# Matmul operand tiles moved to another address modulo 512 bytes by padding two small tiles

## The chip, the cores and the metric

One core of one Trainium2 chip runs the whole program. The metric is the device time of one execution in microseconds (us), as the median of several runs. The profile comes from one further execution with the hardware profiler on.

## What is computed

Two layers of a decoder trunk on 512 tokens with 1024 channels, all in float32. Cut to what matters here:

```python
# layer 0: a state-space head group (A) and a windowed attention head group (B)
hn   = rms_norm(h, mix_norm_w[0]);  proj = hn @ hyb_w_in[0]
y_a  = ssd_mixer(proj[..., :IN_A], ...)              # 1024 wide, gated and normalised
y_b  = swa_sink_attention(proj[..., IN_A:], ...)     # 16 heads of 64
h    = h + concatenate([y_a, y_b]) @ hyb_w_out[0]
# layer 1: a convolution module
h    = h + conformer_conv_module(rms_norm(h, mix_norm_w[1]), ...)
# after each layer, a gated MLP with a causal convolution of width 3
u    = causal_depthwise_conv(rms_norm(h, ffn_norm_w[i]) @ w_up, conv_w, conv_b)   # 1024 -> 5632
h    = h + (silu(u[..., :2816]) * u[..., 2816:]) @ w_down                         # 2816 -> 1024
```

## The kernel before, in words

**Tiling.** Activations lie with channels on the 128 partitions and the 512 tokens along the free axis, so a tile of 128 channels is 128 x 512 floats, 2048 bytes in each partition. A matrix product (`gemm`, L130 to L138) takes one output tile of 128 channels. Each operand is split into a high and a low part of the type fp32r, and a product of two operands is three matmuls of 512 columns that add into one PSUM bank: weights high by activations high (L135), weights high by activations low (L136), weights low by activations high (L137). The weights are the stationary operand, which a LDWEIGHTS brings into the array; the activations are the moving one, which streams past it.

**Weights.** `wload` (L123) fetches 128 x 1024 floats by DMA into `wr`, ScalarE makes the high part `wh` (L119) and VectorE the low part `wl` (L120). There are three buffers of each.

**Phases.** `mix` (layer 0's mixer), `ffn0`, `conf` (the convolution module) and `ffn1` follow each other. Tiles that all phases use (`wr`, `wh`, `wl`, `xr` and some more, L76) live in a pool that stays; each phase opens a pool of its own (L1094 to L1096) on top of it, and gives it back at its end. Inside a pool, tiles lie one after another in the order in which their names first appear, each beginning at a multiple of 32 bytes.

**The moving operands that matter here.** Three names hold them:

- `xr`, 16 tiles in the lasting pool: the normalised activations that enter all up-projections and input projections, and, in the second half of the output projection of `mix`, the operands of head group A (`ya`, L746 to L750).
- `att`, 16 tiles in the pool of `mix`: the split attention output `yb` (L698 to L702), the operands of the first half of that output projection. `out_half` (L754) multiplies one half for one of 8 output tiles: 8 operands x 3 matmuls = 24 matmuls. The first halves of tiles 0 to 4 are done first, in the banks `mm`, `mm`, `mm`, `pa`, `pa`; then the second halves of these, and then for tiles 5 to 7 a first and a second half each.
- `g`, 44 tiles in the pool of an `ffn` phase: the split gated activations (L796 to L799), the operands of the down-projection (L802 to L805). A down-projection has 8 output tiles x 22 operands x 3 = 528 matmuls, and there are two of them. In the phase `conf` the names `g`, `dg` and `u4` hold split operands of the last product (`u4` appears as `u` in the profile).

**Where these tiles lie.** The built program gives every tile a start address in the partition. Taken modulo 512 bytes:

```
tile                          before   with the change
wh, wl (stationary)               32          32
xr                                32          32
att (phase mix)                   64          32
g (phases ffn0 and ffn1)         224          32
g, dg, u4 (phase conf)            32          32
```

A `gemm` takes slices of 128 floats = 512 bytes of `wh` and `wl`, so every stationary slice has the same address modulo 512 as its tile. The pool of a phase begins at 123424 bytes, which is 32 modulo 512. In `ffn0` and `ffn1` its first tile is the table of convolution parameters, 176 floats = 704 bytes, and `g` follows. In `mix` it begins with `rows_t` (2048 bytes), two tiles `sel` (512 bytes each) and `warm` (one float, which takes 32 bytes), and `att` follows; after `att` come the other tiles of the phase (`par_mix`, `pairs`, `halves`, `bc`, `kv`, `xs`, `c`, `a` or `lt`, `b`, `d`, `bt` and small ones).

Of the kernel before, what the change touches and what calls it, by code (L numbers as in the profile page):

```python
# [10 lines left out]
AF = mybir.ActivationFunctionType  # L11
# [3 lines left out]
P = 128  # L15
# [43 lines left out]
def kernel(ctx: ExitStack, tc: tile.TileContext, x, w_in, w_dt, w_out,  # L59
                             pw1, pw2, w_up0, w_up1, w_dn0, w_dn1, par, cst, btab, out):  # L60
    nc = tc.nc
    V, S, G, TE = nc.vector, nc.scalar, nc.gpsimd, nc.tensor
# [16 lines left out]
    def sbt(tag, bufs, n=T, dt=F32, shape=None):  # L79
        pool = sb if tag in base else phase[0]  # L80
        return pool.tile(shape or [P, n], dt, name=nm(tag), tag=tag, bufs=bufs)
# [3 lines left out]
    def bank_of(tag):  # L85
        return ps.tile([P, T], F32, name=nm(tag), tag=tag, bufs=BANKS[tag])
# [5 lines left out]

    def pload(group, pool, queue=nc.scalar):
        a, b = PGROUP[group]
        room = 640 if group == "conf" else b - a
        ptiles[group] = pool.tile([P, room], F32, name=f"par_{group}")[:, : b - a]
        queue.dma_start(ptiles[group], par[:, a:b])

    pload("norm", one)

    def con(name):
# [10 lines left out]
    ones = one.tile([P, P], F32, name="ones")  # L112
# [17 lines left out]
    def gemm(bank, w, ops, first, last):  # L130
        wh, wl = w
        n = len(ops)
        for i, (xh, xl) in enumerate(ops):
            c = slice(i * P, (i + 1) * P)
            TE.matmul(bank, wh[:, c], xh, start=first and i == 0, stop=False)  # L135
            TE.matmul(bank, wh[:, c], xl, start=False, stop=False)  # L136
            end = TE.matmul(bank, wl[:, c], xh, start=False, stop=last and i == n - 1)  # L137
        return end  # L138
# [85 lines left out]
    def mixer(norm, nxt):  # L224
        mk = lambda shape, name, dt=F32: phase[0].tile(shape, dt, name=name)
# [94 lines left out]

        first, ws, banks = [], [], {}
        with tc.manual_schedule():
            warm = mk([P, 1], "warm")
            S.activation(warm, ones[:, 0:1], AF.Exp)
            idle = bank_of("pc")
            for _ in range(9):
                TE.matmul(idle[:, :P], ones, ones, start=True, stop=True)
            wd = sbt("att", 16)[:, : KD * 16].rearrange("p (k m) -> p k m", k=KD)
            S.dma_start(wd, w_dt)
            raws = [sbt("wr", 3, RING) for _ in range(3)]  # L330

            def wpart(i, p):
                if i == len(raws):
                    raws.append(sbt("wr", 3, RING))
                nc.sync.dma_start(raws[i][:, p], w_in[i][:, p])

            lower, upper, whole = slice(0, RING // 2), slice(RING // 2, RING), slice(0, RING)
            xload = lambda k: nc.sync.dma_start(h[k], x[:, k, :])
            xload(0)
            wpart(0, lower)  # L340
            xload(1)
            wpart(0, upper)
            xload(2)
            wpart(1, whole)
            for k in (3, 4, 5):
                xload(k)
            wpart(2, whole)
            for k in (6, 7):
                xload(k)
            wd2 = sbt("att", 16, T, F32R).rearrange("p (k m) -> p k m", k=KD)  # L350
            V.memset(f32(wd2), 0.0)
            V.tensor_copy(wd2, f32(wd2))
            V.tensor_copy(wd2[:, :, 0:16], wd)
            V.tensor_tensor(wd2[:, :, 32:48], wd, f32(wd2[:, :, 0:16]), op=ALU.subtract)

            def split(i, p):
                if len(ws) == i:
                    ws.append((sbt("wh", 3, RING, F32R), sbt("wl", 3, RING, F32R)))
                wh, wl = ws[i]
                S.copy(wh[:, p], raws[i][:, p])  # L360
                V.tensor_tensor(wl[:, p], raws[i][:, p], f32(wh[:, p]), op=ALU.subtract)

            dbank = bank_of("pa")
            first += [bank_of("mm") for _ in range(3)]

            def dt_part(k):
                for i, o in enumerate(norm.ops[k]):
                    TE.matmul(dbank[0:64], wd2[:, k], o, start=k == 0 and i == 0, stop=k == KD - 1 and i == 1)

            def part(i, k):  # L370
                c = slice(k * P, k * P + P)
                gemm(first[i], [w[:, c] for w in ws[i]], [norm.ops[k]], k == 0, k == KD - 1)

            def arrive(k, tiles):
                dt_part(k)
                for i in tiles:
                    part(i, k)

            norm.split(0)
            split(0, lower)  # L380
            arrive(0, (0,))
            norm.split(1)
            norm.square(0, V, "att", 16)
            split(0, upper)
            arrive(1, (0,))
            norm.split(2)
            norm.square(1, V, "att", 16)
            arrive(2, (0,))
            norm.split(3)
            split(1, whole)  # L390
            arrive(3, (0,))
            norm.split(4)
            arrive(4, (0,))
            for k in range(3):
                part(1, k)
            norm.square(2, V, "att", 16)
            norm.split(5)
            arrive(5, (0,))
            norm.square(3, V, "att", 16)
            for k in range(3, 6):  # L400
                part(1, k)
            split(2, whole)
            norm.split(6)
            arrive(6, (0, 1))
            norm.split(7)
            arrive(7, (0, 1))
            for k in range(4, KD):
                norm.square(k, V, "att", 16)
            wpart(3, whole)
            nc.sync.dma_start(ctile, cst)  # L410
            pload("mix", phase[0], nc.sync)
            wpart(4, whole)
            wpart(5, whole)
            norm.reduce()
            split(3, whole)
            dts = sbt("att", 16)[0:64]
            S.copy(dts, dbank[0:64])
            for k in range(6):
                part(2, k)
            norm.spread()  # L420
            for k in (6, 7):
                part(2, k)
# [670 lines left out]
    for i, p in enumerate(phases):  # L1093
        a, b = norms[i], norms[i + 1]  # L1094
        with tc.tile_pool(name=p, bufs=1) as pool:
            phase[0] = pool  # L1096
            if p != "mix":
                pload(p, pool)
            if p == "mix":
                mixer(a, b)  # L1100
            elif p == "conf":
                conformer(a, b)
            else:
                l = int(p[-1])
                ffn(a, b, (w_up0, w_up1)[l], (w_dn0, w_dn1)[l], l)
# [105 lines left out]
```

## Time and profile before

| what | value |
|---|---|
| median of 3 runs | 1307.34 us (1306.35 to 1309.11) |
| the profiled execution | 1305.71 us |
| span in the profile, first to last instruction | 1303.9 us |
| PE (matmul) busy | 1287.4 us |
| PEld (weight load) busy | 1028.8 us |
| DVE / ACT / POOL busy | 855.6 / 514.3 / 123.3 us |
| matmuls in the profile | 6431 |

The profiled execution's own time is 1.63 us under the median of the runs, and its span 1.8 us under its own time. PE is TensorE, DVE VectorE, ACT ScalarE and POOL GpSimd; L135 is line 135 of the kernel. The profile's duration of one matmul runs from its issue to a modelled end, and the matmuls overlap in a pipeline. So the pace of a row of matmuls is read from the distance between two starts, not from the duration.

### The profile page before, as it was taken

Reading aid. Unit: us, or ns where it says so; the run is one execution under the profiler, and the core shown is the slowest. Engines: PE = TensorE matmul, PEld = TensorE weight load, DVE = VectorE, ACT = ScalarE, POOL = GpSimd, SP = SyncE. Lnnn points to the kernel's source line nnn. Section 1 sums busy time; section 2 is a strip of 40 time slices with the busy share of each in tenths; the row PEclk is TensorE's granted clock in tenths of the full one; section 3 lists DMA queues with packets and bytes.
Section 4 is the critical chain, followed back from the end, with each engine's and each line's share of the span. In section 5 each row is a group of like instructions: output and inputs, shape, how many; then the busy total and the mean of one; then the engine's idle time right before and its main releaser. Section 6 shows DMA issues by size and latency. Waiting matters only on the chain.

```text
span 1303.9 us, 16808 instructions
## 1 busy us (share of the span) xinstructions
PE 1287.4 (99%) x6431; PEld 1028.8 (79%) x6431; DVE 855.6 (66%) x1444; ACT 514.3 (39%) x812; POOL 123.3 (9%) x198
## 2 busy tenths in 40 slices
PE   9999999999999999999999999999999999999998
PEld 7878877778888888888888876649888888888886
DVE  7986769985258777777333377757677777773231
ACT  5465547863244333333222231226443333332110
POOL 0032204630210000000000100000500000000000
PEclk9999999999999999999999999999999999999999
DMA  6312221212233333333333265550433333333331
GB/s 223 97 49 65 66 67 64 66 50 81 97 97 88 98 96 97 96 98 92 100 89 90 89 181 149 149 150 2 118 96 97 97 97 97 97 93 99 118 109 35
DMA packets 40113, 125.13 MB, mean 96 GB/s; under 512 B 4704, under 2 KB 5088, under 8 KB 40032
## 3 DMA queue, kind: packets, MB, share of 16 engines
q1 hardware_dynamic: 39312, 123.50, 31.3%
q8 instruction: 51, 0.84, 0.3%
q10 hardware_dynamic: 720, 0.55, 0.2%
q14 instruction: 30, 0.25, 0.1%
HBM read 119.73 MB, written 4.29 MB: 95 GB/s over the span
## 4 chain that ended last, share of the span: by engine, by line
PE 77%; DVE 3%; DMA 1%; issue 1%; POOL 0%; ACT 0%; SPq 0%; ACTq 0%; POOLq 0%
PE mm L135 23%; PE mm L137 23%; PE mm L136 23%; PE pa L889 3%; PE pc L695 1%; PE pa L135 1%; PE pa L137 1%; PE pa L136 1%; PE pb L686 1%; DMA u<-du 0%; PE mm L989 0%; PE mm L990 0%; PE mm L988 0%; PE pb L163 0%; POOL lt L670 0%
## 5 line engine op out<-in xcount | busy, mean ns | idle before, releaser
L135 PE MATMUL mm<-xr,wh 128*128 128x512 f32 x1120 | 439.5, 392 | 0.0
L136 PE MATMUL mm<-xr,wh 128*128 128x512 f32 x1120 | 437.5, 391 | 0.0
L137 PE MATMUL mm<-xr,wl 128*128 128x512 f32 x1120 | 437.5, 391 | 0.0
L119 ACT CAST wh<-wr 128x1024 fp32r<-128x1024 f32 (+1 forms) x178 | 183.6, 1032 | 458.7 <-PE mm L136 414.4
L120 DVE TENSOR_TENSOR wl<-wr,wh 128x1024 fp32r<-128x1024 f32 (+1 forms) x178 | 214.5, 1205 | 158.3 <-ACT wh L119 153.1
L137 PEld LDWEIGHTS mm<-xr,wl 128*128 128x128 f32 x1120 | 210.4, 188 | 43.9 <-issue 0.2
L135 PEld LDWEIGHTS mm<-xr,wh 128*128 128x128 f32 x1120 | 210.7, 188 | 43.6 <-issue 1.6
L136 PEld LDWEIGHTS mm<-xr,wh 128*128 128x128 f32 x1120 | 210.7, 188 | 43.2 <-DVE xr L183 0.4
L136 PE MATMUL mm<-g,wh 128*128 128x512 f32 x360 | 141.8, 394 | 0.0
L221 DVE TENSOR_TENSOR cv<-mm,nrb 128x512 f32<-128x512 f32 x116 | 79.7, 690 | 94.5 <-PE mm L137 90.5
L137 PE MATMUL mm<-g,wl 128*128 128x512 f32 x352 | 138.7, 394 | 0.0
L135 PE MATMUL mm<-g,wh 128*128 128x512 f32 x352 | 138.7, 394 | 0.0
L216 DVE SCALAR_TENSOR_TENSOR ct<-cv,par_ffn,ct 128x510 f32<-128x510 f32 (+1 forms) x176 | 131.0, 747 | 3.5 <-issue 0.4
L136 PEld LDWEIGHTS mm<-g,wh 128*128 128x128 f32 x360 | 67.3, 187 | 16.5
L135 PEld LDWEIGHTS mm<-g,wh 128*128 128x128 f32 x352 | 65.8, 187 | 16.5
L137 PEld LDWEIGHTS mm<-g,wl 128*128 128x128 f32 x352 | 65.8, 187 | 16.2
L193 POOL TENSOR_TENSOR nsum<-nsum,nsq 128x512 f32<-128x512 f32 x21 | 33.6, 1601 | 428.5 <-ACT nsq L192 428.5
L213 ACT ACTIVATE ct<-cv,par_ffn 128x512 f32<-128x512 f32 x88 | 71.3, 812 | 3.2 <-DVE cv L221 3.0
L794 ACT ACTIVATE th<-ct 128x512 f32<-128x512 f32 x44 | 27.8, 632 | 84.5 <-DVE ct L216 84.5
L805 DVE TENSOR_TENSOR h<-h,mm 128x512 f32<-128x512 f32 x16 | 11.0, 688 | 59.0 <-PE mm L137 59.0
L889 PE MATMUL pa<-u,dg 128*32 128x512 f32 (+1 forms) x464 | 46.4, 550 | 2.6 <-DMA u<-du 2.6
L889 PEld LDWEIGHTS pa<-u,dg 128*32 128x32 f32 x464 | 14.7, 114 | 29.4 <-issue 23.0
(308 smaller groups left out, 1387.7 us busy)
## 6 DMA issues: line engine op xcount, KB each, us to landing
wr<-w_up SPq DMA_DIRECT2D x88, 512.0 KB, 3.5
wr<-w_in SPq DMA_DIRECT2D x29, 512.0 KB, 3.6
wr<-w_dn SPq DMA_DIRECT2D x32, 448.0 KB, 3.3
wr<-pw SPq DMA_DIRECT2D x24, 512.0 KB, 5.5
wr<-w_out SPq DMA_DIRECT2D x16, 512.0 KB, 3.6
wr<-w_dn SPq DMA_DIRECT2D x16, 512.0 KB, 3.5
u<-du SPq DMA_DIRECT2D x28, 266.0 KB, 4.6
h<-x SPq DMA_DIRECT2D x8, 256.0 KB, 4.9
```

The lines of the kernel that those rows point to most:

```text
L119: S.copy(wh[:, :n], raw[:, :n])
L120: V.tensor_tensor(wl[:, :n], raw[:, :n], f32(wh[:, :n]), op=ALU.subtract)
L135: TE.matmul(bank, wh[:, c], xh, start=first and i == 0, stop=False)
L136: TE.matmul(bank, wh[:, c], xl, start=False, stop=False)
L137: end = TE.matmul(bank, wl[:, c], xh, start=False, stop=last and i == n - 1)
L193: eng.tensor_tensor(self.sum, self.sum, sq, op=ALU.add)
L213: S.activation(t, v, AF.Identity, bias=bias, scale=w(taps - 1))
L216: V.scalar_tensor_tensor(t[:, s:], v[:, : T - s], w(k), t[:, s:], op0=ALU.mult, op1=ALU.add)
L221: V.tensor_tensor(v, bank, rb, op=ALU.mult)
L686: TE.transpose(tb[:, blk(b * 2 + e)], lt[:, e, blk(b)], ident)
L794: S.activation(sg, c, AF.Silu)
L889: TE.matmul(cv[quad(c), :n], diag[j][:, g, c, :], u4[j][:, c, 4 * g + t0 : 4 * g + t0 + n], start=g == 0, stop=g == npe - 1 and j < 2)
```

## The change

Two tiles are made larger, and nothing else. The parameter table of the two `ffn` phases goes from 176 to 256 floats (704 to 1024 bytes), and `warm` from 1 to 128 floats (512 bytes); what is read and written in them stays the same. In `ffn0` and `ffn1` the tiles behind the table move up by 320 bytes, and in `mix` all tiles behind `warm` move up by 480 bytes. The last byte used goes from 228784 to 229264. Every engine has the same instructions in the same order with the same waits as before.

```diff
@@ def pload
-        room = 640 if group == "conf" else b - a
+        room = 640 if group == "conf" else -(-(b - a) // P) * P if group[:3] == "ffn" else b - a
@@ def mixer
-            warm = mk([P, 1], "warm")
-            S.activation(warm, ones[:, 0:1], AF.Exp)
+            warm = mk([P, P], "warm")
+            S.activation(warm[:, 0:1], ones[:, 0:1], AF.Exp)
```

## Rows read from the trace of the kernel before

**Rows 1.** Page, part 1: busy time of each engine.

```profile
PE 1287.4 (99%) x6431; PEld 1028.8 (79%) x6431; DVE 855.6 (66%) x1444; ACT 514.3 (39%) x812; POOL 123.3 (9%) x198
```

**Rows 2.** Page, part 4: the chain that ended last, by engine and line.

```profile
PE 77%; DVE 3%; DMA 1%; issue 1%; POOL 0%; ACT 0%; SPq 0%; ACTq 0%; POOLq 0%
```

**Rows 3.** PE timeline, both down-projections: start us, duration us, engine, line, operation.

```profile
615.60 0.39 PE L135 MATMUL mm<-g,wh 128*128 128x512 f32 x1
...
738.80 0.39 PE L135 MATMUL mm<-xr,wh 128*128 128x512 f32 x1
...
1176.86 0.39 PE L135 MATMUL mm<-g,wh 128*128 128x512 f32 x1
...
1299.82 0.40 PE L137 MATMUL mm<-g,wl 128*128 128x512 f32 x1
```

**Rows 4.** Busy time by stretch (us, with counts) in four stretches.

```profile
core 0: us, PE busy (x) PEld busy (x) DVE busy (x) ACT busy (x) POOL busy (x), PEclk, DMA share, GB/s
302.42:313.62 11.20, 11.20 (x50) 9.00 (x48) 6.79 (x9) 4.26 (x6) 0.00 (x0) 1.00 0.29 96
329.96:340.84 10.88, 10.88 (x49) 9.01 (x48) 3.83 (x4) 3.27 (x5) 3.52 (x2) 1.00 0.30 98
400.00:600.00 200.00, 200.00 (x884) 165.64 (x884) 156.38 (x205) 77.19 (x92) 0.00 (x0) 1.00 0.32 97
620.00:720.00 100.00, 100.00 (x430) 80.14 (x429) 31.52 (x35) 27.10 (x32) 7.94 (x5) 1.00 0.32 94
```

**Rows 5.** Groups of PE by form, whole span: out<-in count | busy us, mean ns.

```profile
L135 PE MATMUL mm<-xr,wh 128*128 128x512 f32 x1120 | 439.5, 392 | 0.0
...
L137 PE MATMUL mm<-g,wl 128*128 128x512 f32 x352 | 138.7, 394 | 0.0
...
L137 PE MATMUL mm<-att,wl 128*128 128x512 f32 x48 | 19.0, 397 | 0.0
...
L137 PE MATMUL mm<-dg,u 128*128 128x512 f32 x24 | 9.3, 389 | 0.0
...
L137 PE MATMUL pa<-att,wl 128*128 128x512 f32 x16 | 6.3, 395 | 0.0
...
L137 PE MATMUL pa<-xr,wl 128*128 128x512 f32 x16 | 6.2, 389 | 0.0
```

**Rows 6.** PE timeline, start of the output projection of mix.

```profile
280.49 0.48 PE L135 MATMUL mm<-att,wh 128*128 128x512 f32 x1
...
286.17 0.39 PE L135 MATMUL mm<-att,wh 128*128 128x512 f32 x1
288.52 1.13 PE L163 MATMUL pb<-ctile,gr 128*128 128x128 f32 x8 [1.96 <-DVE gr L741]
```

**Rows 7.** DVE timeline, the last operands of group A.

```profile
306.60 1.47 DVE L749 TENSOR_TENSOR xr<-xs,xr 128x512 fp32r<-128x512 f32 x2
```

**Rows 8.** PE timeline, the first matmuls of the second half.

```profile
313.62 0.39 PE L135 MATMUL mm<-xr,wh 128*128 128x512 f32 x1
313.85 0.40 PE L136 MATMUL mm<-xr,wh 128*128 128x512 f32 x1
314.08 0.39 PE L137 MATMUL mm<-xr,wl 128*128 128x512 f32 x1
314.31 0.40 PE L135 MATMUL mm<-xr,wh 128*128 128x512 f32 x1
314.55 0.39 PE L136 MATMUL mm<-xr,wh 128*128 128x512 f32 x1
314.78 0.39 PE L137 MATMUL mm<-xr,wl 128*128 128x512 f32 x1
315.00 0.39 PE L135 MATMUL mm<-xr,wh 128*128 128x512 f32 x1
```

**Rows 9.** Page, part 5: the split of the weights (busy, mean ns | idle before, releaser).

```profile
L119 ACT CAST wh<-wr 128x1024 fp32r<-128x1024 f32 (+1 forms) x178 | 183.6, 1032 | 458.7 <-PE mm L136 414.4
```

**Rows 10.** Groups of PE by form: matmuls on other tiles whose addresses move.

```profile
L686 PE MATMUL pb<-ctile,lt 128*128 128x128 f32 x112 | 19.1, 283 | 1.5 <-POOL lt L670 0.9
...
L479 PE MATMUL pb<-ctile,xs 128*128 128x128 f32 x32 | 5.1, 276 | 0.0
```

**Rows 11.** Groups of ACT by form, 60 to 380 us: squares of three tiles.

```profile
L540 ACT ACTIVATE nsq<-att 128x512 f32<-128x512 f32 x8 | 5.1, 633 | 0.2
...
L192 ACT ACTIVATE nsq<-h 128x512 f32<-128x512 f32 x7 | 4.4, 633 | 0.0
...
L730 ACT ACTIVATE nsq<-xs 128x512 f32<-128x512 f32 x6 | 3.8, 632 | 6.0 <-DVE rsi L142 3.0 <-DVE xs L724 2.9
```

## The prediction

> **What bounds the kernel now.** I read the busy times first, then the chain that ended last, then the pace of the matmuls in single stretches, because the change touches no instruction and can act only through how long an instruction takes. TensorE is busy for 99% of the span [rows 1], and most of the chain that ended last lies on it [rows 2]. In the two down-projections it has no gap: the first one starts its 528 matmuls at 615.60 us and the next product starts at 738.80 us, the second starts at 1176.86 us and its last matmul at 1299.82 us [rows 3]. So what one matmul there costs is one step on the path that sets the end.
>
> That step is not the same everywhere. The first down-projection takes 738.80 - 615.60 = 123.20 us for 528 starts, or 233.3 ns from start to start; the second 1299.82 - 1176.86 = 122.96 us for 527, again 233.3 ns. In the up-projection 884 weight loads fall into 200 us, 226.2 ns each, and in the down-projection 429 into 100 us, 233.1 ns each (a load at an edge counts too, so both are a little low) [rows 4]. The clearest pair lies within the output projection of mix: 48 matmuls on `att` into the banks `pa` take 11.20 us, 233.3 ns each; 48 matmuls on `xr` into the same banks, with weights of the same buffers, some 20 us later take 10.88 us, 226.7 ns each [rows 4]. The granted clock is 1.00 (2.4 GHz) in all four stretches, the DMA share is 0.29 to 0.33, and VectorE is busier where the matmuls are the faster ones in the long pair, so neither the clock nor other work explains the difference.
>
> What does go with it is the address. `xr` lies at the weights' own address modulo 512 bytes, `att` 32 bytes past it and `g` 192 bytes past it. The phase `conf` gives the counter-check: there `g`, `dg` and `u` lie at the weights' address, and the modelled duration of the matmul is 389 ns, as for `xr` in the banks `pa`, against 394 ns for `g` in the ffn phases and 395 to 397 ns for `att` [rows 5]. So the name of the tile, the engine that wrote it and the product do not matter, and equal or unequal address does, in every group of long products that the trace has. I take 233.3 ns as the pace of unequal addresses and 226.7 ns as the pace of equal ones, a difference of 6.6 ns (11.20 - 10.88 = 0.32 us over 48 is 6.67 ns).
>
> **The change part by part.**
>
> *The gated tiles.* Padding the table puts `g` at the weights' address in both ffn phases. The count is 2 x 528 = 1056 matmuls, of which 1055 have a successor's start behind them. At 6.67 ns each this is 7.04 us, half of it in each phase. All of it lies on the path, if the weights keep up: one buffer of 1024 columns serves 24 matmuls, which take 5.60 us now and 5.44 us then, and the split of it takes 1.03 us on ScalarE, whose idle time before that instruction was ended by TensorE giving a buffer back for 414.4 of 458.7 us [rows 9]. The weights wait for TensorE, then, and not the reverse, and the up-projection already runs at the faster pace with the same supply. What is late next is nothing in this stage.
>
> *The attention tiles.* Padding `warm` puts `att` at the weights' address. The output projection has 8 x 24 = 192 matmuls on it. The first 25 of them stand before a wait: they run from 280.49 to 286.17 us and then TensorE idles 1.96 us for `gr` from VectorE [rows 6]. VectorE's chain to `gr` does not depend on these matmuls, so the time won on some 24 of them (0.16 us) only lengthens the wait. The other 168 gain 168 x 6.67 ns = 1.12 us. They bring the start of the second half forward by about 0.6 us, from 313.62 us [rows 8], and its last operand is ready at 306.60 + 1.47 = 308.1 us [rows 7], so 5 us of cover remain and nothing takes the gain back.
>
> *The change of address inside a product.* When the product passes from `att` to `xr`, the first 6 steps of `xr` take 315.00 - 313.62 = 1.38 us instead of 6 x 226.7 ns = 1.36 us, with single steps of 0.22 to 0.24 us before the pace settles [rows 8]. So the pace is something that settles over several matmuls. There are four such passages in the output projection and one after the first down-projection; without them some 0.02 us each is won, 0.1 us together.
>
> *The other tiles of mix.* All of them move by 480 bytes, which is 32 back modulo 512. Pairs that move together keep their distance (keys and queries, `b` with `bc` and `c`, `d` with `bc`); pairs with an operand that stays change it: the transposes by the constant table, 112 records on `lt` and 32 on `xs` [rows 10], and, by my count, some 90 more in groups of 18 or fewer. The trace shows no price for the distance of such short matmuls. Bounded from both sides by the step found above, 144 + 90 = 234 matmuls at 6.67 ns are 1.6 us either way. I take 0, because the transposes of `lt` start from four different addresses modulo 512 and those of `xs` from a fifth, and the two groups differ by only 7 ns in mean duration; both ends go into the range.
>
> *ScalarE, VectorE, GpSimd and the DMAs.* I cost them at nothing. ScalarE's square of a 128x512 tile takes 633, 633 and 632 ns from `att`, `h` and `xs`, which lie at 64, 0 and 384 modulo 512 [rows 11], so its pace does not see the address. In the down-projections VectorE is covered by TensorE in any case (31.5 us busy of 100 [rows 4]); if that cover were gone, a slower VectorE would show first in the mixer. The padding is not read, written or moved.
>
> Sum: 7.04 + 1.12 + 0.1 = 8.3 us. Against the profiled execution's own time this gives 1305.71 - 8.3 = 1297.4 us; that execution stood 1.63 us under the median of the runs, so the median to expect is 1307.34 - 8.3 = **1299.1 us**, 0.63% less.
>
> **The rivals.**
>
> *Nothing changes.* The difference in pace could belong to what distinguishes the stages otherwise, such as the values or the accumulation over 22 operands instead of 8. For it speaks only that no row shows the same tile at two addresses within one stage; against it the pair in the banks `pa` and the phase `conf`. It gives 1307.3 us. The Trainium skill would come out here: "SBUF — State Buffer", section "SBUF: two separate sides", says that "PE, ACT, and DVE's dedicated pair never wait on anyone", and "TensorE: Matmul & The Clock Gate", Part 2, gives TensorE two independent read ports, one for the moving and one for the stationary operand; so no relation of their addresses should cost anything. By that rule the sum would be 0; the two paces in the trace, 226.7 and 233.3 ns at one clock, disagree with it or at least have no place in it.
>
> *Only one of the two parts works.* If equality matters and something else holds `att` up, the time is 1307.3 - 7.0 = 1300.3 us; if the reverse, 1307.3 - 1.2 = 1306.1 us. The first is close to the forecast, and the second would need `g` to behave otherwise in ffn than in conf.
>
> *The pace settles elsewhere, and slower.* A single step at the passage is as long as 0.24 us [rows 8], so a worse rhythm than 233.3 ns exists, at least for a step. `g` comes to lie an odd number of 512 bytes from the weights (124448 - 80928 = 85 x 512), while `xr` lies an even number from them. If the chip sees 1024 bytes and not 512, the down-projections could settle between the two, at some 236.7 ns as an estimate from these rows: 1056 x 3.4 ns = 3.6 us more, 1310.9 us. It decides from a mean step above 233.3 ns. Against it: the 128-column slices of the weights alternate between odd and even distances anyway, and so do those that meet `xr`.
>
> **How the numbers follow.** A measurement of this kernel can tell about 0.2% (2.6 us) from no change. I give the forecast 0.82, the first part alone 0.07, no change or the attention part alone 0.08, and the slower rhythm 0.03. The predicted time is the likeliest, 1299.1 us. The runs lie 1.0 us below and 1.8 us above their median; I take two thirds of that for the spread of a median. The low end takes the 1.6 us of the other tiles as a gain: 1299.1 - 1.6 - 0.7 = 1296.8 us. The high end takes them as a loss, 1299.1 + 1.6 + 1.2 = 1301.9 us, which also holds the first part alone. With 0.89 of the chance in cases that centre within this range and a little of it past the ends, it should hold the time 8 times in 10. Faster by over 0.2%: 0.82 + 0.07 = 0.89. Within 0.2%: 0.08. Slower by over 0.2%: 0.03.
>
> **What would show it.** In the profile after, the first down-projection should take 528 x 226.7 ns = 119.7 us instead of 123.2, the 48 matmuls on `att` in `pa` 10.88 us instead of 11.20, the modelled duration of matmuls on `g` and `att` should fall to 389 ns or so, and the wait for `gr` should grow from 1.96 to about 2.1 us. The up-projections should be as long as before. The prediction is wrong if `g` keeps 233 ns, or if the down-projections gain their 3.5 us each and the mixer up to 280 us gives more than 1.6 us of it back.

## The result, and the profile after

The changed kernel takes 1298.78 us in the median of 4 runs (1298.68 to 1300.18), against 1306.84 us (1306.10 to 1309.11) for the kernel before: a ratio of 0.9938 with a 95% interval from 0.9921 to 0.9955. That is 8.1 us less; 8.3 were forecast. The profiled execution took 1298.77 us, 6.94 us less than that of before.

The two down-projections come first, in the timeline of TensorE in the profile after (start, duration, engine, line, operation). They answer to [rows 3]:

```profile
616.58 0.39 PE L135 MATMUL mm<-g,wh 128*128 128x512 f32 x1
...
736.26 0.39 PE L135 MATMUL mm<-xr,wh 128*128 128x512 f32 x1
...
1173.41 0.39 PE L135 MATMUL mm<-g,wh 128*128 128x512 f32 x1
...
1292.86 0.39 PE L137 MATMUL mm<-g,wl 128*128 128x512 f32 x1
```

The first takes 736.26 - 616.58 = 119.68 us for its 528 steps, 226.7 ns each, where it took 123.20 us. The second takes 119.45 us for 527 steps instead of 122.96. Together they bring 7.03 us.

The busy time by stretch answers to the first two stretches of [rows 4]: 48 matmuls on `att`, then 48 on `xr`, in the same banks. The columns are the same as there:

```profile
304.35:315.23 10.88, 10.88 (x50) 9.01 (x49) 6.79 (x9) 4.27 (x6) 0.00 (x0) 1.00 0.31 98
331.55:342.43 10.88, 10.88 (x50) 9.01 (x49) 3.83 (x4) 3.28 (x5) 3.52 (x2) 1.00 0.30 99
```

The two are equal now; before, the first took 11.20 us. The groups of TensorE by form answer to [rows 5], with the modelled duration of `g` down from 394 to 389 ns and that of `att` in `pa` from 395 to 389 ns:

```profile
L137 PE MATMUL mm<-g,wl 128*128 128x512 f32 x352 | 136.9, 389 | 0.0
...
L137 PE MATMUL pa<-att,wl 128*128 128x512 f32 x16 | 6.2, 389 | 0.0
```

One place went the other way in this execution. The timeline at the first wait for `gr` answers to [rows 6]:

```profile
286.56 0.39 PE L135 MATMUL mm<-att,wh 128*128 128x512 f32 x1
288.98 1.13 PE L163 MATMUL pb<-ctile,gr 128*128 128x128 f32 x8 [2.03 <-DVE gr L741]
...
291.55 0.63 PE L137 MATMUL mm<-att,wl 128*128 128x512 f32 x1
291.98 0.63 PE L135 MATMUL mm<-att,wh 128*128 128x512 f32 x1
...
294.27 0.39 PE L135 MATMUL mm<-att,wh 128*128 128x512 f32 x1
```

The wait grew from 1.96 to 2.03 us, where about 2.1 was forecast. Behind it the matmuls start 0.43 us apart for some 3 us. The granted clock of this stretch is half, 0.50 or 1.2 GHz instead of 2.4:

```profile
290.50:293.90 3.40, 3.40 (x11) 2.82 (x11) 3.14 (x5) 2.09 (x4) 0.00 (x0) 0.50 0.49 154
```

So the two profiled executions must not be subtracted blindly. From the first to the last matmul on `att` the profile after takes 88.42 us, 0.54 more than before, although a matmul on `att` costs less at the full clock. Whether the change provokes the half clock was the first question for the experiments; the second was what "the same address modulo 512" really means.

### The profile page after: what moved, and what is told of

Its sections match the earlier page's. It is cut to its first block, busy times and chain, and to the rows that moved or that the text cites. A ratio compares the mean times of both kernels' runs of the same rounds, so it can differ in the third digit from the quotient of the medians.

```text
span 1297.0 us, 16808 instructions
## 1 busy us (share of the span) xinstructions
PE 1280.2 (99%) x6431; PEld 1031.0 (79%) x6431; DVE 855.2 (66%) x1444; ACT 514.9 (40%) x812; POOL 123.6 (10%) x198
## 4 chain that ended last, share of the span: by engine, by line
PE 78%; DVE 2%; POOL 0%; DMA 0%; issue 0%; ACT 0%; SPq 0%; ACTq 0%; POOLq 0%
PE mm L135 23%; PE mm L136 23%; PE mm L137 23%; PE pa L889 3%; PE pc L695 1%; PE pa L136 1%; PE pa L135 1%; PE pa L137 1%; PE pb L686 1%; DMA u<-du 0%; PE mm L989 0%; PE mm L990 0%; PE mm L988 0%; PE pb L163 0%; POOL lt L670 0%
## 5 line engine op out<-in xcount | busy, mean ns | idle before, releaser
L136 PE MATMUL mm<-xr,wh 128*128 128x512 f32 x1120 | 437.8, 391 | 0.0
L137 PE MATMUL mm<-xr,wl 128*128 128x512 f32 x1120 | 437.6, 391 | 0.0
L137 PEld LDWEIGHTS mm<-xr,wl 128*128 128x128 f32 x1120 | 210.6, 188 | 43.7 <-issue 0.2
L136 PEld LDWEIGHTS mm<-xr,wh 128*128 128x128 f32 x1120 | 210.7, 188 | 42.9 <-DVE xr L183 0.4
L136 PE MATMUL mm<-g,wh 128*128 128x512 f32 x360 | 140.0, 389 | 0.0
L135 PE MATMUL mm<-g,wh 128*128 128x512 f32 x352 | 136.9, 389 | 0.0
L137 PE MATMUL mm<-g,wl 128*128 128x512 f32 x352 | 136.9, 389 | 0.0
L136 PEld LDWEIGHTS mm<-g,wh 128*128 128x128 f32 x360 | 67.6, 188 | 14.1
L137 PEld LDWEIGHTS mm<-g,wl 128*128 128x128 f32 x352 | 66.1, 188 | 13.7
```

## The experiments

All runs compute the full result. Times are medians, and ratios stand against the kernel before on the same chip.

### Each padding alone

Run e1 has only the padded table, e2 only the padded `warm`, and e3 is the changed kernel once more. All edits below are against the changed kernel, cut to the lines that matter.

```diff
# e1_table_only
-            warm = mk([P, P], "warm")
+            warm = mk([P, 1], "warm")
...
# e2_warm_only
-        room = 640 if group == "conf" else -(-(b - a) // P) * P if group[:3] == "ffn" else b - a
+        room = 640 if group == "conf" else b - a
```

> Only the parameter table of the ffn phases is padded: g at the weights' address, att still 32 bytes past it. Theory (equal address modulo 512 gives 226.7 ns a step, unequal 233.3): each down-projection 119.7 us instead of 123.2, the 48 matmuls on att in pa still 11.20 us, 7.0 us less in all, about 1299.8 us against 1306.8. Rival (the gain comes from elsewhere in the phases, such as the clock after the waits): the down-projections keep 123.2 us.

> Only warm is padded: att at the weights' address, g still 192 bytes past it. Theory: 48 matmuls on att in pa take 10.88 us, the down-projections keep 123.2 us, the matmuls bring 1.1 to 1.2 us, so about 1305.6 us. Rival (the change itself provokes the half clock that the profile after shows at 290 to 294 us, by making the wait for gr longer): the half clock is there again in this profile, and the time is that of before or up to 0.5 us more.

> The changed kernel once more, on the chip of the others. Theory: 8.2 us less than before in runs whose clock stretches are alike, 7 to 9 us otherwise; the down-projections 119.7 us each in every profile. If the half clock at 290 us belongs to the change it shows here again; if it comes and goes, it may be missing, and then the mixer ends 0.3 us or more earlier than before instead of later.

Measured: e1 1298.51 us, ratio 0.9929 (0.9904 to 0.9955); e2 1306.38 us, ratio 0.9993 (0.9979 to 1.0007); e3 1299.02 us, ratio 0.9940 (0.9920 to 0.9960); before 1306.65 us (17 runs, 1303.33 to 1311.13). By stretch, e1 has the first down-projection from its first to its last start, and then the 48 matmuls on `att` in `pa`:

```profile
618.80:738.25 119.45, 119.45 (x528) 98.94 (x527) 41.02 (x47) 33.23 (x39) 9.59 (x6) 1.00 0.33 97
...
305.62:316.82 11.20, 11.20 (x49) 9.00 (x48) 6.78 (x9) 4.26 (x6) 0.00 (x0) 1.00 0.29 96
```

And the same two in e2:

```profile
614.56:737.53 122.97, 122.97 (x529) 98.55 (x527) 41.03 (x47) 33.08 (x39) 9.47 (x6) 1.00 0.32 94
...
302.36:313.25 10.89, 10.89 (x49) 9.01 (x48) 6.79 (x9) 4.27 (x6) 0.00 (x0) 1.00 0.30 99
```

Each padding does its own part and nothing else: the table 122.97 to 119.45 us, `warm` 11.20 to 10.89. In the medians all of the gain that can be told from the spread is the table's.

For the half clock, 288 to 296 us, first e1 and then e2 (the granted clock is the third number from the end):

```profile
288.00:296.00 8.00, 7.43 (x27) 6.55 (x28) 6.60 (x14) 3.06 (x5) 0.00 (x0) 0.57 0.19 66
```

```profile
288.00:296.00 8.00, 7.44 (x41) 6.49 (x42) 7.08 (x17) 3.41 (x6) 0.00 (x0) 1.00 0.21 66
```

In e1 the output projection is that of before, and the half clock is there, even longer than in the profile after; in e2 it is that of the change, and the half clock is missing. In e3, which is the changed kernel again, it is there. So it comes without the moved `att` and can be missing with it; the change is not what it needs. Of the 12 profiles of this study that have this wait (before, after and e1 to e10), 9 show it: 4 of the 6 with `att` at the address of `wh` (modulo 256), and 5 of the 6 others. What e2 gives where no half clock intervenes is seen from its first to its last matmul on `att`; the profile before has 87.88 us for this stretch:

```profile
280.57:367.42 86.85, 84.76 (x385) 69.99 (x385) 41.48 (x70) 26.53 (x35) 13.94 (x8) 1.00 0.28 90
```

That is 1.03 us less, where 1.12 and some 0.1 were forecast. The profile of e10, which also has `att` moved and no half clock there, has 86.81 us. The time of the runs cannot show it: the interval of e2 reaches from 2.7 us less to 0.9 more.

The half clock shows something else. In e1, with `att` still 32 bytes past the weights, six steps under it take 295.19 - 292.62 = 2.57 us, 0.43 us each, the same as with `att` at their address in the profile after:

```profile
292.62 0.63 PE L135 MATMUL mm<-att,wh 128*128 128x512 f32 x1
...
295.19 0.63 PE L135 MATMUL mm<-att,wh 128*128 128x512 f32 x1
```

From the starts in the traces, the steps on `att` in this stretch settle at 426 or 427 ns in all 9 profiles, whatever the distance. So the price of an unequal address was seen at the full clock alone.

### Relation or address

```diff
# e4_xr_apart
             def split(i, p):
+                if not ws:
+                    G.memset(sb.tile([P, 8], F32, name="gap"), 0.0)   # between xr and wh
                 if len(ws) == i:
                     ws.append((sbt("wh", 3, RING, F32R), sbt("wl", 3, RING, F32R)))
```

> The changed kernel with a tile of 32 bytes put between xr and wh, and all behind it moved by 32 bytes: wh, wl, g, att, dg and u at 64 modulo 512, xr still at 32, so 32 bytes before the weights. Theory (the relation counts): matmuls on xr slow down to 230 to 233 ns, 3408 of them, 11 to 22 us more than the changed kernel, 1310 to 1321 us; g and att keep 226.7 ns at their new address. Rival (the address of the moving operand alone counts, and 32 is the good one): xr keeps 226.7 ns, and g and att go to 233.3 ns, 1307 us.

Measured: 1319.47 us, ratio 1.0097 (1.0067 to 1.0127). By stretch: the up-projection, the first down-projection, `att` in `pa`, `xr` in `pa`:

```profile
420.00:600.00 180.00, 180.00 (x773) 144.93 (x772) 136.22 (x178) 68.00 (x80) 0.00 (x0) 1.00 0.30 95
...
628.70:748.16 119.46, 119.46 (x528) 98.92 (x527) 41.05 (x47) 33.10 (x39) 9.57 (x6) 1.00 0.33 97
...
308.34:319.22 10.88, 10.88 (x50) 9.01 (x48) 6.79 (x9) 4.26 (x6) 0.00 (x0) 1.00 0.31 99
336.02:347.22 11.20, 11.20 (x49) 9.02 (x48) 3.82 (x4) 3.29 (x5) 3.49 (x2) 1.00 0.29 95
```

`xr`, which did not move, now takes 180 us for 772 weight loads (233.2 ns) and 11.20 us in `pa`; `g` and `att`, at a new address but at the weights' own, keep the fast pace. The relation of the two addresses counts, and the rival of a good address for itself falls. It also shows that the price of a step is the same for `xr` as for `g` and `att`: an unlucky tile of 32 bytes costs 20 us here (1319.47 against the 1299.02 us of e3).

### Which distances are good

In four kernels, the table and `warm` were padded to other sizes, so that each profile has `g` at two distances (one in each ffn phase) and `att` at a third.

```diff
# e5: table {"ffn0": 192, "ffn1": 288}, warm 24    e6: {272, 224}, warm 40
# e7: {248, 264}, warm 56                          e8: {240, 208}, warm 72; the lines of e5:
-        room = 640 if group == "conf" else -(-(b - a) // P) * P if group[:3] == "ffn" else b - a
+        room = 640 if group == "conf" else {"ffn0": 192, "ffn1": 288}.get(group, b - a)
-            warm = mk([P, P], "warm")
+            warm = mk([P, 24], "warm")
```

> g 256 bytes past the weights (modulo 512) in ffn0 and 128 in ffn1, att 96 past them. Theory (512 is the period, only distance 0 is fast): 233.3 ns a step in both down-projections, 123.2 us each, about the time of before. Rivals: with a period of 256 the first down-projection takes 119.7 us; with 128, both do.

> g 64 bytes past the weights in ffn0 and 384 in ffn1, att 160. Theory: 233 ns a step in both, about the time of before. Rival (the price falls off with the distance): one of them lies between 226.7 and 233.3 ns, or under 226.7 ns, which would point to a better place than that of the change.

> g 480 bytes past the weights (32 before them) in ffn0 and 32 in ffn1, att 224. Theory: near misses cost as much as far ones, 233 ns a step in both. Rival (the two streams must only be near each other): 226.7 ns in one or both.

> g 448 bytes past the weights in ffn0 and 320 in ffn1, att 288. Theory: 233 ns a step in both. Rival (distances before the weights differ from those past them): 448 below 233 ns and 320 not, or the reverse.

One run each: 1305.54, 1306.46, 1306.58 and 1305.34 us, against 1309.21 us in one run of the kernel before. The time of the whole says little here; the stretches do, each from the first to the last start of a down-projection, 527 steps. e5, 256 bytes and then 128:

```profile
617.57:737.02 119.45, 119.45 (x528) 98.94 (x527) 41.05 (x47) 33.23 (x39) 9.58 (x6) 1.00 0.33 97
1176.70:1299.66 122.96, 122.96 (x529) 98.93 (x527) 33.70 (x35) 22.30 (x23) 0.00 (x0) 1.00 0.29 90
```

e6, 64 and then 384:

```profile
618.79:739.43 120.64, 120.64 (x529) 99.08 (x527) 41.05 (x47) 33.22 (x39) 9.62 (x6) 1.00 0.32 96
1177.61:1300.58 122.97, 122.97 (x529) 98.97 (x527) 33.72 (x35) 22.27 (x23) 0.00 (x0) 1.00 0.30 90
```

e7, 480 and then 32:

```profile
618.76:741.73 122.97, 122.97 (x529) 99.10 (x528) 41.05 (x47) 33.15 (x39) 9.49 (x6) 1.00 0.32 95
1177.73:1300.70 122.97, 122.97 (x529) 98.91 (x527) 33.70 (x35) 22.28 (x23) 0.00 (x0) 1.00 0.30 90
```

e8, 448 and then 320:

```profile
617.50:740.47 122.97, 122.97 (x529) 98.68 (x527) 41.05 (x47) 33.11 (x39) 9.51 (x6) 1.00 0.32 95
1178.81:1299.45 120.64, 120.64 (x528) 99.07 (x527) 33.71 (x35) 22.36 (x23) 0.00 (x0) 1.00 0.30 91
```

Divided by 527, with 0 from the profile after and 192 from that of before:

```
distance of g from the weights (bytes)     0     32     64    128    192    256    320    384    448    480
ns from start to start                 226.7  233.3  228.9  233.3  233.3  226.7  228.9  233.3  233.3  233.3
```

Three pairs that are 256 apart agree: 0 and 256, 64 and 320, 128 and 384; so do 192 (the kernel before) and 448. The 48 matmuls on `att` in `pa` lie at 96, 160, 224 and 288 bytes in these four kernels and take 11.20, 11.25, 11.20 and 11.20 us; so 32 and 288 agree as well, and 224 and 480. So the period is 256 bytes, not 512, and the theory's "only distance 0" falls: 256 is as good, and 64 costs a third of the price. No distance tried is better than 0, and 32 bytes cost as much as 128 or 192.

### Which load, and how exact

In e9 only `wl` is moved, by 32 bytes; small tiles before and behind it bring everything else back to the address of `wh` modulo 256. In e10 `g` starts some bytes inside a larger tile.

```diff
# e9_wl_apart
-                    ws.append((sbt("wh", 3, RING, F32R), sbt("wl", 3, RING, F32R)))
+                    hi = sbt("wh", 3, RING, F32R)
+                    if not ws: G.memset(sb.tile([P, 8], F32, name="gap0"), 0.0)
+                    ws.append((hi, sbt("wl", 3, RING, F32R)))
+                    if len(ws) == 1: G.memset(sb.tile([P, 56], F32, name="gap1"), 0.0)
-            warm = mk([P, P], "warm")
+            warm = mk([P, 64], "warm")
# e10_near_16_4, for gh and gw
-            gh = sbt("g", 44, T, F32R)
+            gh = sbt("g", 44, T + 64, F32R)[:, (4, 1)[l] : (4, 1)[l] + T]
```

> All moving operands at the address of wh modulo 256 bytes (g and dg 256 past it), only wl 32 bytes past them. Theory (what counts is the weights that are being loaded against the stream that is running, load by load): the load of wl is the one of three at a bad distance, so 226.7 + 6.67 / 3 = 228.9 ns a step in up- and down-projections, some 10 us more than the changed kernel, 1309 us. Rivals: the rhythm settles as in the worst pair, 233 ns, 1330 us; or wl does not matter, 226.7 ns, 1299 us.

> The changed kernel with g starting 16 bytes past the weights' address modulo 256 in ffn0 and 4 bytes past it in ffn1 (a tile of 2304 bytes each, read from its fifth or its second float on). Theory (exact equality): 233 ns a step in both, 1306 us. Rival (a block of some bytes counts, and a start within it is as good): 226.7 ns in one or both, 1299 us if both.

Measured: e9 1326.81 us and e10 1303.82 us, one run each (before 1307.26 us, 11 runs). e9 in the first down-projection, `att` in `pa`, `xr` in `pa`:

```profile
629.51:752.49 122.98, 122.98 (x529) 98.85 (x528) 40.99 (x47) 33.19 (x39) 9.54 (x6) 1.00 0.33 94
...
308.45:319.65 11.20, 11.20 (x50) 9.00 (x48) 6.79 (x9) 4.26 (x6) 0.00 (x0) 1.00 0.30 96
336.45:347.65 11.20, 11.20 (x50) 9.01 (x48) 3.82 (x4) 3.28 (x5) 3.50 (x2) 1.00 0.28 95
```

Here the theory of a price load by load falls: with one weight tile of two out of place, each of these three products takes the full 233.3 ns in the mean, as if both were, which was the first rival's case. (`wl` also lies 32 bytes from `wh` in this run, so it does not tell a distance between the two weight tiles from one between `wl` and the moving tile.) Inside a triple the steps differ, in the timeline:

```profile
700.45 0.40 PE L136 MATMUL mm<-g,wh 128*128 128x512 f32 x1
700.69 0.39 PE L137 MATMUL mm<-g,wl 128*128 128x512 f32 x1
700.91 0.40 PE L135 MATMUL mm<-g,wh 128*128 128x512 f32 x1
701.15 0.40 PE L136 MATMUL mm<-g,wh 128*128 128x512 f32 x1
701.39 0.39 PE L137 MATMUL mm<-g,wl 128*128 128x512 f32 x1
```

The step from L136 to L137, behind whose start the load of `wl` runs, takes 0.24 us both times; over the 352 such steps of the two down-projections it is 239.0 ns, against 232.6 for the one before it and 228.4 for the one behind. That would fit a meeting of the weights' load with the running stream, whose delay carries into the next steps; no run shows it, nor what they would meet at.

e10, 16 bytes and then 4:

```profile
614.80:736.88 122.08, 122.08 (x528) 99.17 (x527) 41.04 (x47) 33.12 (x39) 9.53 (x6) 1.00 0.33 95
1173.21:1297.94 124.73, 124.73 (x529) 98.95 (x527) 33.68 (x35) 22.25 (x23) 0.00 (x0) 1.00 0.29 88
```

16 bytes cost 231.7 ns a step, and 4 bytes 236.7 ns, more than any other distance. So a start within the same small block is not enough, as the rival had it, and neither step is the 233.3 ns of the theory; of the distances tried, 4 bytes is the worst. In this run alone `g` does not begin at a multiple of 32 bytes, and no run separates that from the distance.

### The wait between the products on `att`

```diff
# e11_fill_wait; out_half and OPEN are defined before the loop over g
             V.tensor_scalar(gr, gr, 0.5, None, op0=ALU.mult)
+            if g == 0:
+                for m in range(2):
+                    banks[m] = bank_of(OPEN[m])
+                    out_half(m, 0, yb)
             gb = sbt("bc", 4)
             tok_bcast(gb, gr)
...
         for m, tag in enumerate(OPEN):
+            if m < 2:
+                continue
# e12_fill_att_apart: the same, and
-            warm = mk([P, P], "warm")
+            warm = mk([P, 1], "warm")
```

> The changed kernel with the first halves of output tiles 0 and 1 issued before the broadcast of the first gr, so that 48 matmuls on att stand before that wait instead of 25. Theory (the wait for gr and the half clock behind it are what hides the attention part): no wait at the first gr, no half clock at 288 to 298 us, 2 us and 1.5 to 3 us less than the changed kernel, 1294 to 1297 us. Rival (the second gr now comes late, its chain being behind the first, and the wait and the half clock move there): 1298 to 1300 us.

> The kernel of the filled wait with warm at its old size, so that att lies 32 bytes past the weights again and g stays at their address. Theory (without the wait and the half clock behind it all 192 matmuls on att are on the path): the stretch from the first to the last matmul on att takes 1.2 to 1.4 us more than the 84.52 us with both paddings (192 x 6.67 ns = 1.28 us), about 1296.6 us. Rival (another wait takes up the gain of the attention part): less than 0.6 us more.

Measured: e11 1295.33 us (6 runs, 1293.72 to 1297.56), ratio 0.9911 (0.9893 to 0.9928); e12 1295.21 us (5 runs, 1295.01 to 1296.83), ratio 0.9912 (0.9898 to 0.9925). From the first to the last matmul on `att`, first e11, then e12:

```profile
280.87:365.39 84.52, 84.46 (x386) 70.11 (x385) 41.41 (x70) 26.53 (x35) 13.95 (x8) 1.00 0.29 93
```

```profile
280.89:366.60 85.71, 85.71 (x386) 70.03 (x385) 41.48 (x70) 26.51 (x35) 13.96 (x8) 1.00 0.29 92
```

The wait is gone, the clock is whole, and the stretch takes 84.52 us instead of the 88.42 of the profile after, and 2.33 us less than in e2, which has the wait of 2.03 us but not the half clock. So e11 beats both kernels: 3.5 us under the changed one by the medians of two sets of runs, although the intervals of the two ratios still touch. e12 shows the attention part in its stretch, 85.71 - 84.52 = 1.19 us, where the theory had 1.2 to 1.4 and the rival less than 0.6. The time that was expected of e12, about 1296.6 us, was missed: its median is 1295.21 us and no longer than that of e11. The two medians come from different sets of runs and do not show the attention part.

## Why the prediction was right, step by step

*The pace.* The reading that 233.3 and 226.7 ns are two paces of one product, set by the address, was right. e4 shows it most directly, since there the tile that stood still slowed down and those that moved kept pace.

*The gated tiles.* 7.04 us were forecast, and 3.52 and 3.51 us were found in the two down-projections, 7.03 together. The weights kept up, as argued: no wait of TensorE appeared there. (A buffer serves 24 matmuls for the first of three parts of a down-projection and 21 for the others, L803, not always 24 as the prediction has it; that is still far more than the 1.03 us of a split.)

*The attention tiles and the passages.* 1.2 us were forecast for both. The stretch of e2 gained 1.03 us and the pair e11 and e12 differs by 1.19 us, with all 192 matmuls on the path for 1.28. The size is right within 0.2 us; no run separates the 0.1 us of the passages from it. In the time of the runs it stays unproven, because the runs spread wider than that. The half clock behind the wait, which the prediction did not have, is alone worth more: the stretch from the first to the last matmul on `att` takes 86.85 us in e2, without one, and 88.42 us in the profile after, with one, so 1.6 us. The wait itself took up less than argued: 24 steps before it became 0.10 us shorter, not 0.16, and the wait 0.07 us longer.

*The other tiles, ScalarE, VectorE.* Nothing of them was found. The up-projection of `ffn0` kept its length: from the last matmul on `att` to the first on `g` it is 247.2 us before and after. The mixer up to its first matmul on `att` took 0.49 us more in the profile after (280.98 against 280.49 us), within the 1.6 us of the prediction, and the change need not be its cause: this point comes at 280.55 and 280.89 us in e1 and e12, whose mixers are up to there those of before, and at 280.57 and 280.98 us in e2 and e3, whose mixers are those of the change. So no price of the other tiles stands out from that spread of 0.4 us. What else separates the two profiled executions is the half clock in the mixer, 0.54 us in the net, and, the other way, 0.9 us from the end of the first down-projection to the start of the second, where waits and clock in the convolution module came and went between kernels that are alike there.

*The median.* 1299.1 us were forecast, 1298.78 and 1299.02 us measured in two sets. That it is so close is partly luck, as the kernel before spreads from 1303.33 to 1311.13 us, and e1, without the attention part, has 1298.51 us.

*The rivals.* "Nothing changes" is refuted by e1 and e4. The Trainium skill's "SBUF — State Buffer", section "SBUF: two separate sides", by which TensorE never waits on anyone, and the two independent read ports of "TensorE: Matmul & The Clock Gate", Part 2, would have given this answer; e9 disagrees with it as a rule for time, as moving one stationary tile by 32 bytes costs 6.7 ns on each step in the mean. "Only one of the two parts works" falls by the stretches of e1 and e2; the time of the changed kernel could not have told it from the forecast. The slower rhythm at an odd multiple of 512 bytes did not come: `g` settles at 226.7 ns there. But slower rhythms do exist, 236.7 ns at a distance of 4 bytes.

*Where the reasons fell short.* The prediction took the period to be 512 bytes and spoke of one price for every unequal address. Only three distances were in the trace of before, 0, 32 and 192 bytes, and they could not tell 512 from 256. The period is 256 bytes, and the price depends on the distance: 2.2 ns at 64 bytes, 5.0 at 16, 6.7 at most others, 10.0 at 4. It was also taken as one price at any clock, and at half the clock none was seen. The forecast did not need this, since 0 was its target either way. The padding of the table could be a fifth as large: 768 bytes instead of 1024, 64 bytes more than the 704 of before instead of 320, give the same 119.45 us (e5).

## What to carry to other kernels

Read the pace of long rows of matmuls from start to start, by operand: a product that runs 3% slower than its neighbour at the same clock may have its moving tile at another address, modulo 256 bytes, than its weights, and some padding mends it (64 bytes were enough in e5). It holds the other way round too: a small tile put in the wrong place of a pool cost 20 us here, with no other change than its own memset. Such a gain is worth its number of matmuls on the path times the step, and where it is smaller than the spread that clock and waits give the runs, the stretch in the trace proves it and the median does not.

## What the runs showed of the hardware

- At the full clock (1.00, 2.4 GHz) the pace of fp32r matmuls of 512 columns with a weight load each is 226.7 ns at best in these products, with the moving tile at a distance of 0 or 256 bytes from the weights, and 228.9 to 236.7 ns at others.
- At half the clock (0.50, 1.2 GHz) the pace on `att` was 426 to 427 ns in 9 profiles, with the same at a distance of 0 and of 32 bytes.
- The distance acts on the whole row: with `wl` alone out of place, the mean step was 233.3 ns, as with everything out of place.
- After a wait of 1.91 to 2.03 us of TensorE the granted clock fell to half in 9 of 12 profiles and not in the 3 others. In the profile after it was 0.50 from 290.50 to 293.90 us. With the wait filled (e11 and e12) neither profile shows it there.
